# Turning blocks on 128 partitions and placing their squares by a copy through DRAM, in a hybrid decoder layer

## The chip, the cores and the metric

One Trainium2 chip, one core. The metric is the device time of one execution in microseconds. The kernel before was run three times: 1752.36, 1752.54 and 1753.24 us; the median, 1752.54 us, is what the change is measured against.

## The reference

One decoder layer over 256 tokens of width 2048, in float32:

```
h = rmsnorm(x, attn_norm_w)
proj = h @ w_in                      # q,k,v,o and gates of the mLSTM; q,k,v of the attention; two branch gates
hm = sigmoid(mo) * head_rmsnorm(mlstm(silu(conv(q,k)), v, gates))      # 8 heads
hd = head_rmsnorm(diff_attention(dq, dk, dv))                          # 8 heads, causal
y = sigmoid(gm) * (hm @ w_bm) + sigmoid(gd) * (hd @ w_bd)
x = x + y @ w_out
h = rmsnorm(x, ffn_norm_w)
x = x + (silu(h @ w_gate) * (h @ w_up)) @ w_down                       # hidden width 5632
return rmsnorm(x, final_norm_w)
```

## The kernel before

**Products.** All the weights pass through TensorE once, in one stream of products. A product (class `Product`, function `run`) computes 512 columns for all 256 tokens: two PSUM tiles of 128 tokens x 512 columns, over up to 16 row blocks of 128 of the contraction axis. To keep float32 accuracy each operand is split into a high part (rounded to the type fp32r) and a low part, and a row block costs three matmuls per PSUM tile (function `three`): high x high, high x low weights, low x high weights. So a row block is six matmuls of 128 x 128 x 512.

**Weights.** `Feed.load` brings four row blocks (1 MB) by one DMA of SP's queue into one of three raw tiles; `Feed.split` then makes the parts of two row blocks (a unit): a cast on ScalarE (wh, line 254) and a subtraction on VectorE (wl, line 255). Splits are issued four units ahead of the product (`AHEAD = 4`) into five buffers. The next load is issued when a raw tile has been split to its end.

**Steps between the products.** Everything else is cut into generators (class `Side`). After each row block, `run` calls `side.tick()` once: each active generator makes one step, and `yield n` lets n ticks pass before its next step. Every engine's instructions run in the order in which the program stands, so the ticks set the order by hand. Before a row block is multiplied, `side.until` calls further ticks until the left operand's block is marked ready; that settles the program's order, while the engines wait on semaphores in time.

**Blocks across.** A product leaves tokens on partitions; the next product wants the contraction axis there. `across_task` brings a block of 256 tokens x 512 columns across, for each kind either on TensorE (`transpose_task`) or, if its kind is in `TURN`, by `turn_task`. These are in `TURN` and come through `across_task`: hm1 to hm3, dq and dk (four each), hd3, y (the first three), x1 (the first three), x1last, g (the first ones of each of three parts: 3, 3 and 2) and glast4 (the last ones of the parts with four blocks, two of them). That is 29 turns. q0 and k0 use `turn` from `conv_task` and are not touched by the change.

`turn` (line 170 on) transposes on VectorE in squares of 32 x 32. An instruction stays within 32 input and 32 output partitions, so there are 16 of them, `rate` per tick (2, and 4 for x1last and glast4):

```
for n in range(16):
    a, b = n // 4, n % 4
    i = src[32 * a:32 * a + 32].rearrange(...)[:, :, :, b]
    o = t[32 * b:32 * b + 32].rearrange(...)[:, :, :, a]
    nc.vector.transpose(out=o, in_=i)
    if n % rate == rate - 1:
        yield
```

Then `turn_task` splits the turned tile into the high part (ScalarE, line 189, or line 195 where a norm's weight scales it) and the low part (VectorE, line 190 or 196), two row blocks per tick, and marks the block ready.

**Where a block is wanted soonest.** Three places have little room. The last block of x1 (x1last) is made behind the product wo3 and is wanted in row block 12 of the very next product, fg0. The last g of a part (glast4) is made behind fu3 or fu7 and is wanted in row block 12 of the next product, fd00 or fd10. All other turned blocks have at least one whole product in between.

**Queues and buffers.** Weight loads, the loads of x and the output go by SP's queue. POOL only sets constants and copies small columns (lines 694 and 695, at the end of an mv product). The turned tiles, the operands' parts and most other tiles of 128 x 1024 share the 25 buffers of the pool c4p.

Of the kernel before, what the change touches and what calls it, by code (L numbers as in the profile page):

```python
# [15 lines left out]
P = 128  # L16
S = 256
# [19 lines left out]
AHEAD = 4  # L37
ORDER = (
# [8 lines left out]
def hybrid_block(ctx, tc, x, attn_norm_w, w_in, conv_w, conv_b, b_igate, b_fgate, mlstm_norm_w,  # L47
                 lambda_q1, lambda_k1, lambda_q2, lambda_k2, diff_norm_w, w_branch_m, w_branch_d,
                 w_out, ffn_norm_w, w_ffn_gate, w_ffn_up, w_ffn_down, final_norm_w, out):
    """One stream of matrix products on the tensor engine; everything else is cut into steps that are  # L50
    issued between them. Every engine's instructions run in the order in which they stand here."""
# [8 lines left out]
    smp = ctx.enter_context(tc.tile_pool(name="smp", bufs=4))  # L60
    accp = ctx.enter_context(tc.tile_pool(name="accp", bufs=4, space=PS))
# [15 lines left out]
    # ---------------------------------------------------------------- steps between the products  # L77
    class Side:
        """Tasks are generators; each yields the number of further ticks to wait before its next step."""
# [35 lines left out]
    # ---------------------------------------------------------------- operands  # L115
    class Split:
        """An operand with its contraction axis on partitions: [P, 4, S] blocks, high and low parts."""
# [13 lines left out]
    def three(o, a, b, first, last):  # L131
        """o += a.T @ b by the products of their parts."""
        nc.tensor.matmul(o, lhsT=a[0], rhs=b[0], start=first, stop=False)  # L133
        nc.tensor.matmul(o, lhsT=a[0], rhs=b[1], start=False, stop=False)  # L134
        nc.tensor.matmul(o, lhsT=a[1], rhs=b[0], start=False, stop=last)  # L135

    def transpose_half(src, dst, g, pr, scale_col=None):
        """Two [S, 128] column blocks src(tt, j) into dst's row blocks, split."""
# [33 lines left out]
    def turn(src, t, rate=2):  # L172
        """t [P, 4, S] = the transpose of src [P, TT, 512], by blocks of 32 x 32 on the vector engine."""
# [8 lines left out]
    def turn_task(src, dst, g, scale_col=None, rate=2):  # L182
        yield 1
        t = c4([P, 4, S], "turned")
        yield from turn(src, t, rate)
        hi, lo = dst.alloc(g)
        for k in range(0, 4, 2):
            if scale_col is None:
                nc.scalar.copy(out=hi[:, k:k + 2], in_=t[:, k:k + 2])
                nc.vector.tensor_tensor(out=lo[:, k:k + 2], in0=t[:, k:k + 2], in1=hi[:, k:k + 2].bitcast(F32),  # L190
                                        op=ALU.subtract)
            else:
                for j in (k, k + 1):
                    sc = scale_col(4 * g + j)
                    nc.scalar.activation(out=hi[:, j], in_=t[:, j], func=AF.Identity, scale=sc)
                    nc.vector.scalar_tensor_tensor(out=lo[:, j], in0=t[:, j], scalar=sc, in1=hi[:, j].bitcast(F32),
                                                   op0=ALU.mult, op1=ALU.subtract)
            if k == 0:
                yield
        yield  # L200
        dst.ready[g] = True

    # ---------------------------------------------------------------- the products and their weights
    class Product:
        """PSUM tiles [128 tokens, 512] of xt.T @ w[rows of kts, c0:c0+512]; done(acc) takes them."""
# [7 lines left out]
    class Feed:  # L213
        """Loads of four row blocks, then splits of two, in the order of the products."""
# [56 lines left out]
    def run(p):  # L271
# [3 lines left out]
        for tts in ([(0,), (1,)] if p.by_token else [(0, 1)]):  # L275
            for u in p.units:
# [4 lines left out]
                for i, kt in enumerate(kts):  # L281
# [6 lines left out]
                    if p is first and kt == 0:  # L288
                        # in the order in which the parts come
# [12 lines left out]
    # ---------------------------------------------------------------- 1 / sqrt  # L302
    def rsqrt(v, n, name):
        """1 / sqrt(v) on [P, n], by Newton steps from an integer estimate."""
# [32 lines left out]
    # ---------------------------------------------------------------- start: constants, x, first weights  # L337
# [7 lines left out]
    def load_x(c, i, n):  # L345
        """Piece i of n of column chunk c of the tokens."""
# [5 lines left out]
    def x_cols(c, k):  # L352
        """Columns [128 k, 128 k + 128) of chunk c."""
# [15 lines left out]
    mask_st = cp.tile([P, S], F32, name="mask_st")   # keys on partitions, queries along the row  # L369
    mask_ts = cp.tile([P, P], F32, name="mask_ts")   # queries on partitions, keys along the row  # L370
# [18 lines left out]
    def warm_up(n):  # L389
        """Products of zeros: the tensor engine's clock rises only under load."""  # L390
# [57 lines left out]
    # ---------------------------------------------------------------- evictions  # L448
# [6 lines left out]
    def values_of(acc, hi, lo):  # L455
        """The product times the token scale, as high and low parts [P, TT, 2, DV]."""
# [10 lines left out]
    # ---------------------------------------------------------------- gates of the mLSTM  # L467
# [12 lines left out]
    def gates_task():  # L480
# [9 lines left out]
        # columns per row block: [i high | f high | i low | f low], 32 apart  # L490
# [9 lines left out]
        # the token scales along the row  # L500
# [23 lines left out]
        # log sigmoid(z) = min(z, 0) - log(1 + exp(-|z|))  # L524
# [10 lines left out]
        # m_t - b_t = max(0, max over s <= t of (ig_s - b_s))  # L535
# [19 lines left out]
    # ---------------------------------------------------------------- mLSTM  # L555
# [150 lines left out]
    # ---------------------------------------------------------------- branch gates and the first branch  # L706
# [15 lines left out]
    # ---------------------------------------------------------------- lambda  # L722
# [349 lines left out]
```

## Time and profile before

| what | value |
|---|---|
| runs | 1752.36, 1752.54, 1753.24 us |
| profiled execution: span from first to last instruction | 1750.4 us |
| TensorE (PE) busy | 1739.8 us |
| TensorE's weight loads (PEld) busy | 1443.0 us |
| VectorE (DVE) busy | 1217.4 us |
| ScalarE (ACT) busy | 856.6 us |
| GpSimd (POOL) busy | 6.3 us |
| moved by DMA | 332.08 MB |

The page gives the profiled execution by its span alone; the 2.1 us between span and median lie around the first and the last instruction. Busy time counts instructions in execution. Shares are of the span. Matmuls overlap by their pipeline, so the mean of one is longer than the distance between two.

### The profile page before, as it was taken

What the parts mean: (1) busy time and instruction counts of PE and PEld (TensorE: products, weight loads), DVE (VectorE), ACT (ScalarE), POOL (GpSimd) and SP (SyncE); (2) the same over time, 40 slices, a digit from 0 to 9 for tenths busy, and PEclk for the clock granted to TensorE, in tenths of its full rate; (3) what the DMA queues carried; (4) which work ended last, traced back from release to release, by engine and by line L of the source; (5) the groups of instructions that cost most, each with busy time, mean ns of one, the idle gap of its engine ahead of it and who ended that gap; (6) DMA issues with size and microseconds to landing.
All of it is one profiled execution on the core that took longest, in us unless ns stands there. A gap on an engine that the chain in (4) does not pass through costs nothing.

```text
span 1750.4 us, 20353 instructions
## 1 busy us (share of the span) xinstructions
PE 1739.8 (99%) x7873; PEld 1443.0 (82%) x7873; DVE 1217.4 (70%) x1838; ACT 856.6 (49%) x1103; POOL 6.3 (0%) x31
## 2 busy tenths in 40 slices
PE   9999999999999999999999999999999999999998
PEld 7888888888888888888888888888888888888886
DVE  6876877875567978876597886666546666546655
ACT  7555565644345555565444554444344444344443
POOL 1000000000000000000000000000000000000000
PEclk9999999999999999999999999999999999999999
DMA  8656555655666556555666566665566665566553
GB/s 265 215 174 192 163 174 172 180 192 195 193 194 179 175 167 187 169 172 181 212 217 204 192 206 203 193 192 193 193 194 192 194 196 195 194 193 195 196 185 106
DMA packets 169872, 332.08 MB, mean 190 GB/s; under 512 B 7584, under 2 KB 9264, under 8 KB 169776
## 3 DMA queue, kind: packets, MB, share of 16 engines
q1 hardware_dynamic: 169744, 330.78, 59.8%
q8 instruction: 61, 1.00, 0.2%
q14 instruction: 35, 0.29, 0.0%
q10 hardware_dynamic: 32, 0.01, 0.0%
HBM read 328.67 MB, written 2.10 MB: 189 GB/s over the span
## 4 chain that ended last, share of the span: by engine, by line
PE 99%; DMA 0%; DVE 0%; SPq 0%; ACT 0%; issue 0%; DVEq 0%
PE acc_fd L135 5%; PE acc_fg L134 5%; PE acc_fg L133 5%; PE acc_fu L134 5%; PE acc_fu L133 5%; PE acc_fd L133 5%; PE acc_fu L135 5%; PE acc_fg L135 5%; PE acc_fd L134 5%; PE acc_mv L133 2%; PE acc_mo L133 2%; PE acc_dq L133 2%; PE acc_gm L133 2%; PE acc_gd L133 2%; PE acc_dq L135 2%; PE acc_dk L135 2%
## 5 line engine op out<-in xcount | busy, mean ns | idle before, releaser
L255 DVE TENSOR_TENSOR wl_fg<-wr_fg,wh_fg 128x1024 fp32r<-128x1024 f32 x88 | 107.8, 1225 | 85.3 <-ACT wh_fg L254 84.7
L255 DVE TENSOR_TENSOR wl_fu<-wr_fu,wh_fu 128x1024 fp32r<-128x1024 f32 x88 | 107.6, 1225 | 80.8 <-ACT wh_fu L254 80.3
L254 ACT CAST wh_fg<-wr_fg 128x1024 fp32r<-128x1024 f32 x88 | 93.0, 1057 | 142.1 <-PE acc_fu L135 66.5
L255 DVE TENSOR_TENSOR wl_fd<-wr_fd,wh_fd 128x1024 fp32r<-128x1024 f32 x82 | 100.1, 1225 | 89.7 <-ACT wh_fd L254 89.6
L254 ACT CAST wh_fd<-wr_fd 128x1024 fp32r<-128x1024 f32 x82 | 86.2, 1056 | 122.1 <-PE acc_fd L135 96.1
L254 ACT CAST wh_fu<-wr_fu 128x1024 fp32r<-128x1024 f32 x88 | 92.6, 1054 | 96.4 <-PE acc_fg L135 48.5
L133 PE MATMUL acc_fg<-wh_fg,x1Th 128*128 128x512 f32 x352 | 136.9, 389 | 0.0
L134 PE MATMUL acc_fg<-wl_fg,x1Th 128*128 128x512 f32 x352 | 136.9, 389 | 0.0
L135 PE MATMUL acc_fg<-wh_fg,x1Tl 128*128 128x512 f32 x352 | 136.9, 389 | 0.0
L133 PE MATMUL acc_fu<-wh_fu,x1Th 128*128 128x512 f32 x352 | 136.9, 389 | 0.0
L134 PE MATMUL acc_fu<-wl_fu,x1Th 128*128 128x512 f32 x352 | 136.9, 389 | 0.0
L135 PE MATMUL acc_fu<-wh_fu,x1Tl 128*128 128x512 f32 x352 | 136.9, 389 | 0.0
L133 PEld LDWEIGHTS acc_fg<-wh_fg,x1Th 128*128 128x128 f32 x352 | 66.1, 188 | 13.7
L135 PEld LDWEIGHTS acc_fg<-wh_fg,x1Tl 128*128 128x128 f32 x352 | 66.1, 188 | 13.7
L133 PEld LDWEIGHTS acc_fu<-wh_fu,x1Th 128*128 128x128 f32 x352 | 66.1, 188 | 13.7
L135 PEld LDWEIGHTS acc_fu<-wh_fu,x1Tl 128*128 128x128 f32 x352 | 66.1, 188 | 13.7
L134 PEld LDWEIGHTS acc_fu<-wl_fu,x1Th 128*128 128x128 f32 x352 | 66.1, 188 | 13.7
L134 PEld LDWEIGHTS acc_fg<-wl_fg,x1Th 128*128 128x128 f32 x352 | 66.1, 188 | 13.6
L178 DVE STREAM_TRANSPOSE turned<-g 32x256 f32<-32x256 f32 x160 | 69.7, 435 | 2.5
L255 DVE TENSOR_TENSOR wl_bm<-wr_bm,wh_bm 128x1024 fp32r<-128x1024 f32 x32 | 39.2, 1225 | 37.4 <-ACT wh_bm L254 37.3
L178 DVE STREAM_TRANSPOSE turned<-tok_dqk 32x256 f32<-32x256 f32 x128 | 55.7, 435 | 2.1
L254 ACT CAST wh_bm<-wr_bm 128x1024 fp32r<-128x1024 f32 x32 | 33.8, 1056 | 46.6 <-PE acc_bm L135 42.4
(378 smaller groups left out, 4611.4 us busy)
## 6 DMA issues: line engine op xcount, KB each, us to landing
wr_fg<-in_w_ffn_gate_dram SPq DMA_DIRECT2D x44, 1024.0 KB, 5.2
wr_fu<-in_w_ffn_up_dram SPq DMA_DIRECT2D x44, 1024.0 KB, 5.2
wr_fd<-in_w_ffn_down_dram SPq DMA_DIRECT2D x44, 1024.0 KB, 5.1
wr_mo<-in_w_in_dram SPq DMA_DIRECT2D x16, 1024.0 KB, 5.5
wr_mv<-in_w_in_dram SPq DMA_DIRECT2D x16, 1024.0 KB, 5.4
wr_gm<-in_w_in_dram SPq DMA_DIRECT2D x16, 1024.0 KB, 5.4
wr_bm<-in_w_branch_m_dram SPq DMA_DIRECT2D x16, 1024.0 KB, 5.1
wr_dq<-in_w_in_dram SPq DMA_DIRECT2D x16, 1024.0 KB, 5.4
```

The lines of the kernel that those rows point to most:

```text
L133: nc.tensor.matmul(o, lhsT=a[0], rhs=b[0], start=first, stop=False)
L134: nc.tensor.matmul(o, lhsT=a[0], rhs=b[1], start=False, stop=False)
L135: nc.tensor.matmul(o, lhsT=a[1], rhs=b[0], start=False, stop=last)
L178: nc.vector.transpose(out=o, in_=i)
L254: nc.scalar.copy(out=hi[:, i:i + step], in_=r)
L255: nc.vector.tensor_tensor(out=lo[:, i:i + step], in0=r, in1=hi[:, i:i + step].bitcast(F32), op=ALU.subtract)
```

## The change

`turn_task` no longer calls `turn`. It transposes all 128 partitions at once, one instruction per 128 tokens, which turns each 32 x 32 square where it lies: the squares then stand in the wrong groups of 32 partitions. One DMA of POOL's queue writes this tile (4 KB per partition) to a tile in DRAM, and four DMAs of the same queue, one for each group of 32 partitions, read the squares back to their places, in pieces of 1 KB. Seven ticks later (`yield TURN_WAIT`) the parts are made as before; since the squares of one row block now lie 32 elements apart, the cast reads them in that order. Scaled blocks get one more tile: ScalarE scales into it, then casts it, and VectorE subtracts from it. `rate` is no longer used by `turn_task`. The other lines of the change only take out comments.

```
+TURN_WAIT = 6
+    drp = ctx.enter_context(tc.tile_pool(name="drp", bufs=3, space=bass.MemoryType.DRAM))
     def turn_task(src, dst, g, scale_col=None, rate=2):
         yield 1
-        t = c4([P, 4, S], "turned")
-        yield from turn(src, t, rate)
+        y = c4([P, 4, 4, TT, 32], "turned")
+        for tt in range(TT):
+            nc.vector.transpose(out=y[:, :, :, tt].rearrange("p b k s -> p k b s"),
+                                in_=src[:, tt].rearrange("p (k b f) -> p k b f", k=4, f=32))
+            yield
+        d = drp.tile([4, 32, 4, 256], F32, tag="d", name="across")
+        nc.gpsimd.dma_start(out=d.rearrange("a f b n -> (a f) (b n)"), in_=y.rearrange("p b k t s -> p (b k t s)"))
+        t = c4([P, 4, 4 * TT, 32], "across")
+        for b in range(4):
+            nc.gpsimd.dma_start(out=t[32 * b:32 * b + 32].rearrange("p a u s -> p a (u s)"),
+                                in_=d[:, :, b].rearrange("a f n -> f a n"))
+        yield TURN_WAIT
         hi, lo = dst.alloc(g)
+        z = None if scale_col is None else c4([P, 4, S], "scaled")
         for k in range(0, 4, 2):
+            def i(k, n):
+                return t[:, :, TT * k:TT * (k + n)].rearrange("p a u s -> p u a s")
+            def o(x, k, n):
+                return x[:, k:k + n].rearrange("p k (t a s) -> p (k t) a s", t=TT, s=32)
             if scale_col is None:
-                nc.scalar.copy(out=hi[:, k:k + 2], in_=t[:, k:k + 2])
-                nc.vector.tensor_tensor(out=lo[:, k:k + 2], in0=t[:, k:k + 2], in1=hi[:, k:k + 2].bitcast(F32),
-                                        op=ALU.subtract)
+                nc.scalar.copy(out=o(hi, k, 2), in_=i(k, 2))
+                nc.vector.tensor_tensor(out=o(lo, k, 2), in0=i(k, 2), in1=o(hi, k, 2).bitcast(F32), op=ALU.subtract)
             else:
                 for j in (k, k + 1):
-                    sc = scale_col(4 * g + j)
-                    nc.scalar.activation(out=hi[:, j], in_=t[:, j], func=AF.Identity, scale=sc)
-                    nc.vector.scalar_tensor_tensor(out=lo[:, j], in0=t[:, j], scalar=sc, in1=hi[:, j].bitcast(F32),
-                                                   op0=ALU.mult, op1=ALU.subtract)
+                    nc.scalar.activation(out=o(z, j, 1), in_=i(j, 1), func=AF.Identity, scale=scale_col(4 * g + j))
+                nc.scalar.copy(out=hi[:, k:k + 2], in_=z[:, k:k + 2])
+                nc.vector.tensor_tensor(out=lo[:, k:k + 2], in0=z[:, k:k + 2], in1=hi[:, k:k + 2].bitcast(F32),
+                                        op=ALU.subtract)
             if k == 0:
                 yield
         yield
         dst.ready[g] = True
```

## Rows read from the trace of the kernel before

**Rows 1.** The page: busy time, granted clock by slices, chain that ended last

```profile
PE 1739.8 (99%) x7873; PEld 1443.0 (82%) x7873; DVE 1217.4 (70%) x1838; ACT 856.6 (49%) x1103; POOL 6.3 (0%) x31
...
PEclk9999999999999999999999999999999999999999
...
PE 99%; DMA 0%; DVE 0%; SPq 0%; ACT 0%; issue 0%; DVEq 0%
```

**Rows 2.** The waits of TensorE, all: us in total, times, longest

```profile
PE ps_warm L393 <- DVE ssx L387: 1.1, 1, 1.1
PE acc_mq L292 <- ACT wh_mq L254: 0.4, 1, 0.4
PE ps_x L401 <- DMA x<-in_x_dram: 0.2, 1, 0.2
```

**Rows 3.** The turned tile's transposes, of g: duration ns min/median/max, first and last start

```profile
L178 DVE STREAM_TRANSPOSE turned<-g x160: 425/436/442, 1071.1 to 1647.4; 32x256 f32<-32x256 f32 x160
```

**Rows 4.** In time order around the start of fd00 (VectorE, then TensorE): start us, length us

```profile
1200.54 1.23 DVE L255 TENSOR_TENSOR wl_fd<-wr_fd,wh_fd 128x1024 fp32r<-128x1024 f32 x1 [1.50 <-ACT wh_fd L254]
1201.68 3.57 DVE L178 STREAM_TRANSPOSE turned<-g 32x256 f32<-32x256 f32 x8
...
1211.30 1.29 DVE L190 TENSOR_TENSOR gT0l<-turned,gT0h 128x512 fp32r<-128x512 f32 x2
...
1196.53 0.39 PE L133 MATMUL acc_fd<-wh_fd,gT0h 128*128 128x512 f32 x1
...
1212.85 0.39 PE L133 MATMUL acc_fd<-wh_fd,gT0h 128*128 128x512 f32 x1
1213.08 0.39 PE L134 MATMUL acc_fd<-wl_fd,gT0h 128*128 128x512 f32 x1
1213.31 0.39 PE L135 MATMUL acc_fd<-wh_fd,gT0l 128*128 128x512 f32 x1
```

**Rows 5.** Groups by line and shape, ScalarE and VectorE: busy us, mean ns, idle before

```profile
L189 ACT CAST gT0h<-turned 128x512 fp32r<-128x512 f32 x8 | 4.6, 623 | 8.2 <-DVE turned L178 8.2
L195 ACT ACTIVATE x1Th<-turned,nw 128x256 fp32r<-128x256 f32 x16 | 7.0, 501 | 8.3 <-DVE turned L178 8.3
L190 DVE TENSOR_TENSOR gT0l<-turned,gT0h 128x512 fp32r<-128x512 f32 x8 | 5.1, 685 | 0.0
L196 DVE SCALAR_TENSOR_TENSOR x1Tl<-turned,nw,x1Th 128x256 fp32r<-128x256 f32 x16 | 6.7, 480 | 0.0
```

**Rows 6.** In time order around the start of fg0 (VectorE, then TensorE)

```profile
1027.66 3.57 DVE L178 STREAM_TRANSPOSE turned<-x 32x256 f32<-32x256 f32 x8
...
1039.23 0.39 PE L135 MATMUL acc_fg<-wh_fg,x1Tl 128*128 128x512 f32 x1
```

**Rows 7.** DMA: GB/s in 40 slices of 1195 to 1215 us; issues, KB, us to landing

```profile
GB/s 242 0 0 0 20 41 188 418 406 410 406 209 0 0 0 33 20 254 397 401 414 422 156 0 0 0 0 0 0 0 0 0 0 0 16 49 127 397 406 406
...
DMA packets 169872, 332.08 MB, mean 190 GB/s; under 512 B 7584, under 2 KB 9264, under 8 KB 169776
...
x<-in_x_dram SPq DMA_DIRECT2D x6, 512.0 KB, 6.2
...
nwa<-in_attn_norm_w_dram ACTq DMA_DIRECT2D x1, 8.0 KB, 3.0
...
DMA to landing us min/median/max: 2.4/3.1/3.3
```

The last line is that of the eight stores of 256 KB to out_dram, from the view of line 959.

**Rows 8.** What an issue on SP's queue takes (ns), and POOL's instructions, by form

```profile
L237 SPq DMA_DIRECT2D wr_bd<-in_w_branch_d_dram x16: 367/368/368, 827.9 to 908.4; - x16
...
L694 POOL CAST vah<-one 128x4 fp32r<-128x4 f32 x8 | 1.6, 200 | 208.2 <-PE ps_at L135 158.0 <-issue 50.2
...
L484 POOL TENSOR_SCALAR_AFFINE_SELECT sel<-sel 8x1024 f32<-8x1024 f32 x1 | 1.1, 1083 | 0.1
L483 POOL MEMSET sel<- 8x1024 f32 x1 | 0.9, 942 | 0.0
```

**Rows 9.** ScalarE's longest wait in all: us in total, times, longest

```profile
ACT wh_fd L254 <- PE acc_fd L135: 96.1, 59, 1.7
```

## The prediction

> **What bounds the kernel now.** I read the page first, then the waits of the tensor engine, then the turned tile, then the time order at the places where a turned block is needed soonest.
>
> The page's busy line and its chain say one thing: TensorE is busy for 1739.8 of 1750.4 us, and 99% of the chain that ended last is TensorE's own matmuls [rows 1]. VectorE's 70% and ScalarE's 49% lie beside that. TensorE's waits confirm it: three of them in the whole program, 1.7 us together [rows 2]. The clock line grants 9 tenths or more in every slice [rows 1], so there is nothing to win there either. In time order the first matmul of fd00 starts at 1196.53 and the one twelve row blocks later at 1212.85 [rows 4]: 1.36 us for a row block of six matmuls, with no gap. The 10.6 us in which TensorE is idle lie at the start and behind the last matmul, where no block is turned by the code that changes.
>
> So a faster VectorE buys nothing. The change can cost time only by making TensorE wait. The profiled span is 1750.4 us, the median of the runs 1752.54, 2.1 us around it; I add to the median.
>
> **What it removes and adds on the engines.** There are 29 turns in turn_task: 10 of g, 8 of the attention's queries and keys, 4 of x1, 3 of hm, 3 of y, 1 of hd; the ten of g are the 160 transposes of [rows 3]. Each loses 16 transposes of 0.436 us, 6.98 us of VectorE, and gets two of 128 x 512. No row shows such a one. A transpose of 256 columns takes 0.436 us, so 0.87 is the upper bound by doubling; a subtraction of 128 x 512 takes 0.685 [rows 3, 5], the lower. I take 0.7 since the row nearest in shape is the subtraction. That leaves 29 x 5.6 = 161 us less VectorE work, all of it beside TensorE: worth 0. The final casts and subtractions are as many as before, with runs of 32 elements; I cost them as now. For the 8 scaled turns (hm, hd, x1) ScalarE writes a scaled tile first (0.50 us per row block, [rows 5]) and then copies it, two more casts of 0.62 us per turn, while VectorE has two subtractions of 0.69 in place of four of 0.48. Covered by the idle ScalarE, except at x1last, below.
>
> **What it adds on the path of the data.** Between the transposes and the cast there is now a store of 512 KB to DRAM and four loads of 128 KB, all five on POOL's queue; the loads wait there for the store. POOL's queue holds little else: the small copies of vah and val at the end of an mv product, which come 12 row blocks or more ahead of the next turn's transfers. SP's queue issues nothing for it, but the weight loads share the 16 DMA engines with it: 30 MB more on 332 MB [rows 7].
>
> How long may this trip, R, take? A block of the last product before a new stage is needed soonest: glast4 (twice) and x1last. The tick order is exact in the code. The task yields once, transposes at the ticks of row blocks 2 and 3, issues the transfers at 4, waits TURN_WAIT = 6 and casts from row block 11; TensorE needs the result at row block 12, and a deadline of 12 holds in time as well.
> - glast4: VectorE reaches the transposes at 1201.68 [rows 4]; two of 0.7 end at 1203.1. Row block 12 starts at 1212.85 and its third matmul, the first that reads the low part, at 1213.31. After the landing come a cast of 0.62 and a subtraction of 0.69 [rows 5]. R is free up to 1213.31 - 1.31 - 1203.1 = 8.9 us. Before, the low parts came at 1211.30 to 1212.59 [rows 4], already only 0.7 us ahead.
> - x1last: transposes from 1027.66, so ended at 1029.06; the third matmul of row block 12 at 1039.23 [rows 6]. Behind the landing lie two scalings (0.50 each), a cast of 0.62, a subtraction of 0.69 [rows 5]: 2.3 us. R is free up to 1039.23 - 2.3 - 1029.06 = 7.9 us.
>
> Each us beyond is a us of TensorE, since nothing else can fill it: cost = 2(R - 8.9) + (R - 7.9) = 3R - 25.7.
>
> **R from both sides.** POOL has not issued a transfer in this trace. Store: 256 KB took 3.1 us from issue to landing (2.4 at least), alone [rows 7]; 256 KB more at the 400 GB/s that the DMA engines reach [rows 7] is 0.65, so 3.75. A weight load of 1 MB runs in bursts of 2.6 us; in the window of glast4 one runs from 1203.5 to 1206.3 [rows 7], over the store, and sharing with it adds up to 1.3 us. At x1last the final norm's weights and a weight load do the same. So 5.05. Loads: 8 KB landed after 3.0 us [rows 7], 128 KB adds 0.3; the four are issued in line, so three issues come ahead of the last. SP takes 0.37 us for an issue [rows 8]; POOL writes its own descriptors, and its costliest instructions here take 0.94 and 1.08 us [rows 8]. I take 0.7, between the two, as POOL is neither. Store 5.05 + 0.35 (the dearer issue) = 5.4; three issues 2.1; last load 3.3 + 0.35 + 0.65 (half a collision with the next weight load, which VectorE now releases sooner, at about 1207) = 4.3. R = 11.8. Lowest: 3.75 + 3 x 0.37 + 3.3 = 8.2, no collision and SP's issue. Highest: two transfers behind a weight load as the 512 KB load of x (6.2, [rows 7]), POOL's 1.08 for each of five issues: 6.2 + 6.2 + 5 x 1.08 = 17.8.
>
> The Trainium skill, "DMA: Bandwidth & Descriptors", section "Anatomy of one DMA — SWDGE (gpsimd) path", fits such a transfer by 2.0 us plus bytes at 436 GB/s. By it the store is 3.2, a last load 2.3, and with three issues R would be near 7 and the sum 0. The trace's 3.1 for 256 KB, where the fit gives 2.6, speaks against the fit as a whole.
>
> The sum: 3 x 11.8 - 25.7 = 9.7 us. 1752.5 + 9.7 = **1762.2 us**.
>
> **Why the other 26 turns cost nothing.** ScalarE and VectorE work in program order, so a cast that waits for its landing holds the weight splits behind it. These run four units ahead: ScalarE waits for TensorE to release the buffer 59 times, 96.1 us, in fd alone [rows 9]. Four units are 8 row blocks, 10.9 us, less the 2.3 of a split itself: a stall of some 8 us passes, and ScalarE at half load catches up. At R = 11.8 the cast of a turn waits about 3 us. The blocks themselves are needed a whole product (16 row blocks, 21.8 us) or more after the product that made them: dk's before the scores behind dv (R up to about 16), y[0..2], x1[0..2] and the other g's later still. If R passed 17 these covers go too.
>
> **Rivals.**
> 1. *Hidden.* R is at most 9.7, so the three waits sum to no more than 3.5 us: 1752.5 to 1756. For it: the lowest bound of 8.2, and the burst that ends at 1206.3 need not meet the store. Against: three issues and two receipts in sequence. It decides at fd00 and fd10 (R = 8.9). 0.25. The Trainium skill's fit, above, lies here.
> 2. *POOL starved.* VectorE's instructions hold up the writing of descriptors: each of five issues waits for a 1.23 us subtraction of wl (1.50 us idle ahead of one, [rows 4], so not always). Full price 6.1 us on R: 3 x 17.9 - 25.7 = 28 us, 1780; half of it 1771. For it: VectorE runs one every 2.7 us at these places. Against: POOL's small copies in this trace take 0.2 us each [rows 8], no stretch. 0.13. The Trainium skill, "SBUF — State Buffer", section "Who interferes with whom", has the shared port between the two; it holds that two-input subtractions block only POOL's reads, which would make this cheap. No run so far shows which.
> 3. *Buffers.* y, the returned tile and, where scaled, one more tile come from the 25 c4 buffers. By count 23 are live at glast4, up to 24 in the attention stage: a load might wait for a buffer. Some us at most; 0.03, within the range.
> 4. *Faster.* Only TensorE's 1.7 us of waits could go, and none lies on this code: 0.02.
>
> **Numbers.** A measurement of this kernel can tell about 0.2%, 3.5 us. Forecast 0.57, hidden 0.25, starved 0.13, buffers 0.03, faster 0.02: faster 0.02, same 0.25, slower 0.73. The range goes from the hidden case's floor, 1752.2, to R = 15.5 (half of rival 2, or the upper bound cut by a third of its way), 3 x 15.5 - 25.7 = 20.8, 1773.5. The likeliest case alone: R from 9.7 to 13.5, 1756 to 1767.5.
>
> **What would show it.** In the profile after: two transposes of 128 x 512 near 0.7 us per turn, VectorE's busy time down by about 160 us; POOL's queue with 145 issues; in TensorE's waits three entries for x1Tl, gT0l and gT1l of 2 to 5 us each, and next to none elsewhere; ScalarE's casts waiting for a DMA named across. Wrong, if TensorE still shows 1.7 us of waits (then R is under 9), if its waits lie in the weights wh or wl (then the covers are gone), or if the transfers land late because POOL's issues spread by more than 1 us each.

## The result and the profile after

After: 1802.88 us, the median of three runs (1797.91 to 1806.84); before 1752.54. The ratio is 1.0284 with an interval of 1.0256 to 1.0311. The forecast was 1762.2 with a range up to 1773.5: the sign is right, and the loss is 50 us where 9.7 were forecast.

The page of after, whose profiled span is 1801.1 us: busy time, granted clock by slices, chain that ended last.

```profile
PE 1754.3 (97%) x7873; PEld 1451.1 (81%) x7873; DVE 1048.9 (58%) x1416; ACT 856.5 (48%) x1119; POOL 85.9 (5%) x176
...
PEclk9999999999999999999999999999999999999999
...
PE 77%; issue 11%; DMA 7%; ACT 2%; DVE 1%; POOL 1%; SPq 0%; ACTq 0%; DVEq 0%; POOLq 0%
```

VectorE lost 168.5 us of work [rows 1], about the 161 forecast, and the kernel gained nothing from it. DMA and "issue" have come into the chain, where TensorE alone stood before. TensorE itself is busy 14.5 us longer with the same 7873 matmuls. Its waits, all of 2 us and more and one of the small ones (us in all, times, longest), for the three entries of [rows 2]:

```profile
PE acc_fg L135 <- ACT x1Th L216: 11.6, 1, 11.6
PE acc_fd L135 <- ACT gT0h L211: 7.6, 1, 7.6
PE ps_tr L145 <- DVE sgd L873: 4.0, 2, 3.0
PE acc_fd L135 <- ACT gT1h L211: 2.8, 1, 2.8
PE acc_fg L135 <- ACT wh_fg L275: 2.6, 1, 2.6
PE ps_at L624 <- DVE nm L628: 2.3, 1, 2.3
PE ps_at L135 <- ACT dkh L211: 2.0, 1, 2.0
...
PE acc_fg L136 <- DVE wl_fg L276: 0.8, 1, 0.8
```

With the other small entries they make 37.9 us, 36.2 more than before. 36.2 of waits and 14.5 of longer matmuls are the 50.7 us between the spans, 1801.1 - 1750.4; nothing is left over. The three urgent blocks (x1Th, gT0h, gT1h) are the first, second and fourth line, 22.0 us. The other 14.2 us lie, but for 0.8 at the start, where the prediction had cost nothing: at weights (wh_fg, wl_fg, wl_gd), at the y transposes (sgd), in the mLSTM (nm) and the attention (dkh).

The 14.5 us are TensorE's clock: its mean over the execution is 0.999 before and 0.989 after, and 0.010 of 1801 us would be some 18 us (an estimate; part of that lies in the waits themselves). Stretches of after behind the waits at fg0 and fd00; the columns are PE, PEld, DVE, ACT and POOL busy (instructions), granted clock, DMA share, GB/s:

```profile
1072.00:1076.00 4.00, 2.99 (x7) 2.37 (x8) 2.52 (x3) 3.30 (x6) 0.00 (x0) 0.50 0.00 0
1076.00:1080.00 4.00, 4.00 (x18) 3.25 (x18) 1.31 (x2) 2.43 (x3) 0.00 (x0) 0.98 0.02 4
1256.00:1260.00 4.00, 3.53 (x8) 2.78 (x9) 2.52 (x3) 1.89 (x3) 0.00 (x0) 0.50 0.00 0
```

When TensorE came back from 11.6 and from 7.6 us of idleness, the granted clock was 0.50, 1.2 GHz of 2.4: seven matmuls in 3.0 busy us and eight in 3.5, where the row after fg0's holds eighteen in 4.0. The 40 slices of the page, 45 us each, don't show it; only narrow windows do.

The turned tile and its trip, from the views of the transposes' line and of the two issue lines: duration in ns min/median/max, first and last start; under the loads, us from issue to landing. They answer to [rows 3, 8].

```profile
L190 DVE STREAM_TRANSPOSE turned<-g x20: 669/686/705, 1107.0 to 1688.1; 128x512 f32<-128x512 f32 x20
...
L195 POOL DMA_DIRECT2D across<-turned x29: 558/558/740, 258.0 to 1689.1; - x29
...
DMA to landing us min/median/max: 4.9/6.0/7.2
...
L198 POOL DMA_DIRECT2D across<-across x116: 550/550/562, 265.4 to 1696.5; - x116
...
DMA to landing us min/median/max: 2.8/4.5/8.3
```

At fd00 and fg0, in time order (start, length), for [rows 4, 6]; POOL, then ScalarE, then TensorE:

```profile
1239.12 0.56 POOL L195 DMA_DIRECT2D across<-turned  x1 [34.19 <-DVE turned L190]
1244.73 1.10 POOL L198 DMA_DIRECT2D across<-across  x2 [5.05 <-ACT wh_fd L275]
1248.19 1.10 POOL L198 DMA_DIRECT2D across<-across  x2 [2.37 <-issue]
...
1255.80 0.62 ACT L211 CAST gT0h<-across 128x512 fp32r<-128x512 f32 x1 [8.57 <-DMA across<-across]
...
1256.47 0.80 PE L135 MATMUL acc_fd<-wh_fd,gT0h 128*128 128x512 f32 x1 [7.61 <-ACT gT0h L211]
...
1029.79 0.56 POOL L195 DMA_DIRECT2D across<-turned  x1 [17.51 <-DVE turned L190]
...
1045.16 0.91 ACT L215 ACTIVATE scaled<-across,nw 128x256 f32<-128x256 f32 x2 [12.57 <-DMA across<-across]
...
1056.31 0.56 POOL L195 DMA_DIRECT2D across<-turned  x1 [18.98 <-DVE turned L190]
...
1071.40 0.91 ACT L215 ACTIVATE scaled<-across,nw 128x256 f32<-128x256 f32 x2 [11.57 <-DMA across<-across]
```

From the store's issue to the first cast or scaling: 16.7 us at fd00, 15.1 at fg0. The lines at 1029.79 and 1045.16 are one of the 26 other turns, x1[2]: ScalarE stood 12.6 us waiting for its landing, then did four weight casts in one run (3.9 us from 1049.0), SP's loads followed in a bunch, and the DMA engines ran at about 400 GB/s nearly throughout 1055 to 1067 us, just when x1last's trip had to pass. Here one trip delays the next by way of the splits.

The same lines show a second effect. At fd00 ScalarE was at its cast 8.1 us behind the store's issue (1255.80 - 8.57 - 1239.12). At x1[2] it was catching up after the hold of the turn before (7.8 us, until 1018.6), ran through the splits in between faster than TensorE uses them, and was at its scaling only 2.8 us behind the issue: of a trip of 15.4 us it waited 12.6. A tick is a place in the order and not a time.

ScalarE's waits for landings (us in all, times, longest) show that this was no single case. Rows 5's casts had waited for transposes; these wait for the DMA:

```profile
ACT scaled L215 <- DMA across<-across: 60.4, 8, 12.6
ACT dkh L211 <- DMA across<-across: 25.7, 4, 11.1
ACT gT0h L211 <- DMA across<-across: 20.4, 4, 8.6
ACT dqh L211 <- DMA across<-across: 18.6, 4, 7.7
ACT yTh L211 <- DMA across<-across: 17.8, 3, 9.5
ACT gT1h L211 <- DMA across<-across: 15.7, 4, 4.9
ACT gT2h L211 <- DMA across<-across: 6.7, 2, 3.4
```

29 waits, one for every turn, 165.3 us: the six ticks of `TURN_WAIT` (the cast comes on the seventh) were too few for each of them. Of the 26 turns that are not urgent, 17 held ScalarE for 3.2 to 4.9 us, and no wait of TensorE follows these. The small waits of TensorE follow five of the nine holds of 6.2 us and more (hm 6.4, dk 11.1, hd 7.4, y 9.5, x1[2] 12.6).

### The profile page after: what moved, and what is told of

Read it like the earlier page. It is cut to its first block, busy times and chain, and to the rows that moved or that the text cites. A ratio compares the mean times of both kernels' runs of the same rounds, so it can differ in the third digit from the quotient of the medians.

```text
span 1801.1 us, 20295 instructions
## 1 busy us (share of the span) xinstructions
PE 1754.3 (97%) x7873; PEld 1451.1 (81%) x7873; DVE 1048.9 (58%) x1416; ACT 856.5 (48%) x1119; POOL 85.9 (5%) x176
## 4 chain that ended last, share of the span: by engine, by line
PE 77%; issue 11%; DMA 7%; ACT 2%; DVE 1%; POOL 1%; SPq 0%; ACTq 0%; DVEq 0%; POOLq 0%
PE acc_fu L136 4%; PE acc_fu L137 4%; PE acc_fu L135 4%; PE acc_fd L135 4%; PE acc_fd L137 4%; PE acc_fd L136 4%; PE acc_fg L135 4%; PE acc_fg L136 4%; PE acc_fg L137 4%; DMA across<-across 3%; DMA across<-turned 3%; PE acc_mo L135 2%; PE acc_mo L137 2%; PE acc_mo L136 2%; PE acc_bd L135 1%
## 5 line engine op out<-in xcount | busy, mean ns | idle before, releaser
L135 PE MATMUL acc_fg<-wh_fg,x1Th 128*128 128x512 f32 x352 | 138.6, 394 | 14.2 <-ACT x1Th L216 11.6
L195 POOL DMA_DIRECT2D across<-turned x29 | 16.4, 565 | 1416.6 <-DVE turned L190 1416.6
L135 PEld LDWEIGHTS acc_fu<-wh_fu,x1Th 128*128 128x128 f32 x352 | 66.1, 188 | 13.7
L137 PEld LDWEIGHTS acc_fu<-wh_fu,x1Tl 128*128 128x128 f32 x352 | 66.1, 188 | 13.7
L198 POOL DMA_DIRECT2D across<-across x116 | 63.2, 552 | 175.5 <-DMA across<-turned 97.5
L135 PE MATMUL acc_fd<-wh_fd,gT0h 128*128 128x512 f32 x128 | 50.8, 397 | 7.6 <-ACT gT0h L211 7.6
```

The costliest lines, as they stand in the source:

```text
L195: nc.gpsimd.dma_start(out=d.rearrange("a f b n -> (a f) (b n)"), in_=y.rearrange("p b k t s -> p (b k t s)"))
L198: nc.gpsimd.dma_start(out=t[32 * b:32 * b + 32].rearrange("p a u s -> p a (u s)"), in_=d[:, :, b].rearrange("a f n -> f a n"))
```

## The experiments

The theories on record before the first four runs: A, a trip of some 15 us is paid where its block is wanted in the next product, by casts held behind a landing, and by half the clock behind each wait; B, the extra traffic or POOL's queue slows the weight loads everywhere; C, the strided casts and the scaled tile cost. The table holds what before, after and the thirteen kernels of the experiments gave: the median, the ratio to before with its interval, TensorE's busy time and waits in the profiled run, and ScalarE's waits for landings of "across". The profiled run of e5 is one of its longest (1758.0 us), that of e11 took 1759.8.

| kernel | us | ratio [interval] | TensorE busy, us | its waits, us | ScalarE's waits for landings, us (times) |
|---|---|---|---|---|---|
| before | 1752.5 | | 1739.8 | 1.7 | |
| after | 1802.9 | 1.0284 [1.0256, 1.0311] | 1754.3 | 37.9 | 165.3 (29) |
| e1 three old | 1782.6 | 1.0169 [1.0147, 1.0192] | 1748.7 | 21.0 | 148.0 (26) |
| e2 eleven ticks | 1774.6 | 1.0128 [1.0113, 1.0143] | 1746.1 | 18.3 | 19.4 (5) |
| e3 both | 1752.6 | 1.0003 [0.9993, 1.0012] | 1740.3 | 2.1 | 2.5 (2) |
| e4 no trip | 1753.5 | 1.0008 [0.9999, 1.0018] | 1741.2 | 1.7 | none |
| e5 direct copies | 1754.0 | 1.0018 [1.0008, 1.0027] | 1742.3 | 5.1 | 5.3 (2) |
| e6 SP's queue | 1762.6 | 1.0061 [1.0046, 1.0076] | 1743.1 | 10.7 | 14.7 (6) |
| e7 filled waits | 1774.0 | 1.0123 [1.0106, 1.0140] | 1758.3 | 7.4 | 24.4 (4) |
| e8 quiet trips | 1752.3 | one run | 1739.8 | 1.9 | 0.6 (1) |
| e9 four more | 1758.0 | 1.0035 [1.0022, 1.0047] | 1739.2 | 7.7 | 19.8 (4) |
| e10 q1, k1 too | 1768.0 | 1.0088 [1.0074, 1.0101] | 1741.7 | 15.7 | 34.7 (7) |
| e11 eight ticks | 1760.8 | 1.0059 [1.0035, 1.0083] | 1742.5 | 6.6 | 64.4 (25) |
| e12 direct, POOL | 1764.0 | 1.0066 [1.0052, 1.0080] | 1745.4 | 7.7 | 11.5 (6) |
| e13 twenty ticks | 1748.8 | 0.9980 [0.9971, 0.9989] | 1736.5 | 1.6 | 2.1 (1) |

**Which turns cost (e1 to e4).** e1 turns the three urgent blocks by the old sixteen transposes; e2 lengthens the wait of the 26 others; e3 does both; e4 leaves the five transfers out.

```diff
-        if kind in TURN:
+        if kind in LAST:                      # e1: x1last, glast4
+            yield from old_turn_task(tile, dst, g, scale_col, rate)
+        elif kind in TURN:
             yield from turn_task(tile, dst, g, scale_col, rate)
```

> The three last turns (x1last, glast4 twice) use the old sixteen transposes again, the other 26 keep the trip through DRAM. Theory A (the trip is some 15 us long; it is paid where a block is wanted in the next product, by ScalarE's casts held behind a landing, and by the half clock after each wait): the waits of 25 us at fg0, fd00 and fd10 and their half clock go; left are the waits elsewhere (mlstm, ylast, dk, about 10 us) and two short stretches at half clock, about 5 us: 1764 to 1770 us. Theory B (the extra traffic and POOL's queue slow the weight loads everywhere): nearly all of the loss stays, 1790 us or more.

Measured: 1782.6, above what A had for it and below B's. A's mechanism stands, its size does not: the 26 turns held to be covered cost 28.2 us of span by themselves (1778.6 - 1750.4), 19.3 of waits and 8.9 of longer matmuls.

```diff
-            yield from turn_task(tile, dst, g, scale_col, rate)
+            yield from turn_task(tile, dst, g, scale_col, rate, TURN_WAIT if kind in LAST else 11)
...
-        yield TURN_WAIT
+        yield wait
...
-            side.push("tr", across_task("x1" if c < 3 else "x1last", t, x1T, c, ffn_col, 2 if c < 3 else 4))
+            side.push(f"tr{c}", across_task("x1" if c < 3 else "x1last", t, x1T, c, ffn_col, 2 if c < 3 else 4))
```

(y and the attention's queries and keys get a lane per task in the same way.)

> The trip for all 29 turns, but the 26 that are not last ones wait 11 ticks more instead of 6 before their casts, and turns that would overlap in a lane get lanes of their own. Theory A: the waits outside fg0, fd00 and fd10 go, and at fg0 the wait is shorter since x1's third turn no longer pushes the last one back: three waits of 3 to 8 us with the half clock after each, 1772 to 1784 us. Theory B: no change, 1795 us or more.

Measured: 1774.6. Of TensorE's waits only the three urgent ones are left besides those at the start, with 9.9 (x1Th), 4.6 (gT0h) and 2.3 us (gT1h). So the urgent turns alone cost 22 us (against e3, below): 16.8 of waits, some 6 of half clock. With e1's 28.2 that is nearly the whole of the 50.7.

> Both: the old transposes for the three last turns, the trip with 11 ticks for the other 26. Theory A: no wait of TensorE is left but the 1.7 us of before, 1751 to 1755 us, with VectorE some 145 us less busy than before: the relief is worth nothing. Theory B: 1775 us or more, since the traffic is as in the change but for a tenth.

Measured: 1752.6, the time of before, with 26 trips and 27 MB of extra traffic in it. B falls.

```diff
-        d = drp.tile([4, 32, 4, 256], F32, tag="d", name="across")
...
-        yield TURN_WAIT
+        t = y.rearrange("p b k t s -> p b (k t) s")
+        yield TURN_WAIT
```

> The change without its five transfers: the casts read the tile that the two transposes wrote, so the squares are not placed (that part of the computation is left out). Everything else as in the change, with the strided casts and the extra scaled tile. Theory A: 1751 to 1755 us, as the kernel before. A theory C, that the strided casts or the extra scaled tile cost: 1760 us or more.

Measured: 1753.5. C falls, and with it any worth of the relief: VectorE at 1053.6 us and not 1217.4 [rows 1] leaves the time where it was.

**How long must the wait be (e11).** e3 with 8 in place of 11.

> As the run with the old form of the three urgent turns and eleven ticks of wait for the others, with eight ticks in place of eleven. A trip takes 11.4 to 16.3 us in the traces, eight ticks are 10.9 us behind the store's issue, eleven are 15.0. Theory A (what the 26 covered turns cost at six ticks, 8.2 us, is ScalarE and VectorE held behind landings that come after the tick, and the splits queued behind them): at eight ticks most holds are a few us and inside the splits' lead, 1752 to 1760 us. Rival H (not the length of the wait but the separate lanes took the cost of six ticks away): 1752 to 1753.5 us, as at eleven.

Measured: a median of 1760.8, in runs from 1752.9 to 1776.7; A's range ended at 1760. Rival H falls, since the lanes are e3's: the ticks count. ScalarE's waits for landings are 148.0, 64.4 and 2.5 us at 6 (e1), 8 and 11 ticks. Six ticks with the lanes were not run, so what the lanes gave of the step from e1 to e11 is not shown. At eight, whether a landing comes in time differs from run to run, and the time with it.

**Why the trip is long (e5, e6, e8, e12).** e5 takes e2 and moves the squares of the three urgent turns in one hop; e6 takes e2 and issues the three urgent trips on SP's queue; e8 puts two trips that nothing reads into e3, behind the last weight loads; e12 is e5 with another share of the queues.

```diff
+        if direct:
+            for a in range(4):
+                for b in range(4):
+                    queue = nc.gpsimd if b < 2 else nc.sync
+                    queue.dma_start(out=t[32 * b:32 * b + 32, a].rearrange("p u s -> p (u s)"),
+                                    in_=y[32 * a:32 * a + 32, b].rearrange("p k t s -> p (k t s)"))
```

> As the run with eleven ticks of wait, but in the three turns that the next product wants (the last x1 and the two last g) the squares go straight from the turned tile to their places in on-chip memory, by sixteen copies of 32 KB (eight on POOL's queue, eight on SP's) and not by a store to DRAM and four loads behind its landing: one landing in place of two. In the run with eleven ticks these three trips took 16.3, 13.7 and 11.4 us from the store's issue to the first cast that reads the squares, and TensorE waited 9.9, 4.6 and 2.3 us for them. Theory A (the length of the trip, two landings one behind the other, is what the three products wait for): one landing of 4 to 6 us behind issues of 3 to 4.4 us makes 8 to 10 us, which the 7.9 to 8.9 us of free room nearly hold; waits of 0 to 2 us each, 1752 to 1762 us. Rival B (the two queues' many small copies land as late as the trip, since the weight loads hold the DMA engines): 1770 us or more.

Measured: 1754.0, in A's range (runs from 1753.9 to 1758.1). In the profiled one, of 1758.0, fd00 and fd10 no longer wait; 3.3 us are left at fg0, more than A's 0 to 2, where the first scaling starts 10.6 us behind the first copy's issue.

> As the run with eleven ticks of wait, but the three turns that the next product wants have their store and loads issued on SP's queue, not on POOL's. Rival D (the trip is long because POOL prepares its descriptors itself: in the traces POOL stands 2.4 us between two loads of one trip, and waits about 5 us for the store): the trip falls to 10 us or less and the time to 1762 us or less. Theory A (the trip is two landings beside weight loads that fill the DMA engines, whichever queue issues it): 12 us or more each, 1770 to 1780 us; SP's weight loads behind the waiting loads then come up to 5 us later, which the splits' lead of four units (10.9 us) holds.

Measured: 1762.6, between the two, at D's edge. The trips fell from 16.3, 13.7 and 11.4 us to 12.7, 10.3 and 10.4; this is fg0's (SP, then ScalarE), with the loads' KB and median us to landing at fg0, first e6's, then e2's:

```profile
1031.90 0.33 SPq L197 DMA_DIRECT2D across<-turned  x1
1040.33 1.76 SPq L200 DMA_DIRECT2D across<-across  x4
...
1044.56 0.91 ACT L217 ACTIVATE scaled<-across,nw 128x256 f32<-128x256 f32 x2 [6.95 <-DMA across<-across]
...
across<-across SPq DMA_DIRECT2D x4, 128.0 KB, 2.8
...
across<-across POOLq DMA_DIRECT2D x4, 128.0 KB, 5.4
```

A trip is 2.7 us shorter on the mean of the three, but that is not the price of POOL's queue. The stores landed no sooner on SP: after 8.4, 5.9 and 6.0 us (fg0, fd00, fd10), where e2's took 8.7, 4.9 and 4.9. The loads did, after 2.8 to 2.9 us and not 5.4, 4.4 and 4.3. SP's next weight loads stood in the queue behind these loads (at fg0 they were issued at 1042.19), so the loads hardly shared the DMA engines. This rival to D was not tested by a run of its own. Even here fg0's store takes 8.4 us before its loads can be issued.

> The run with the old form of the three turns and eleven ticks of wait for the others, and two more trips of a 512 KB tile that nothing reads, after the last weight load has landed (in the trace of before the DMA engines move nothing from about 1719 to 1737 us): one issued on POOL at about 1720 us, one on SP at about 1736 us. It measures a trip by itself. Theory A (a good part of the 11.4 to 16.3 us is shared DMA engines): 8 to 10 us from the store's issue to the last landing on either queue, stores of 3 to 4.5 us. Rival D (POOL's own preparation is what is long): 11 us or more on POOL, and 3 us or more shorter on SP. The time stays at 1751 to 1758 us.

Measured: the two issue lines of the loads ("still" is the tile they fill), first POOL's, then SP's.

```profile
L962 POOL DMA_DIRECT2D still<-across x4: 552/553/557, 1721.5 to 1723.1; - x4
L972 SPq DMA_DIRECT2D still<-across x4: 346/425/432, 1731.8 to 1733.1; - x4
...
DMA to landing us min/median/max: 2.8/2.9/2.9
```

POOL's store was issued at 1715.1 and landed after 6.1 us; its last load landed at 1723.1 + 2.9 = 1726.0: 10.9 us. SP's store was issued at 1729.0, so 2.8 us passed until its loads: 1733.1 + 2.9 - 1729.0 = 7.0 us. So a bare trip is 7 us on SP, and some 4 us more come with the weight loads beside it (e6's mean of 11.1), as A says in kind; its 8 to 10 us on either queue met neither trip. The 10.9 us look like rival D, but POOL's trip was not a bare one: its store shared the DMA engines with the last weight load, of 1 MB, for most of its 6.1 us, and 3.6 of the 3.9 us between the two trips lie ahead of the loads. The loads, on quiet engines, landed after 2.8 to 2.9 us on both queues, and the shortest of POOL's stores in e2 took 3.1 us. What these runs show of POOL's queue by itself is an issue every 0.55 us where SP's come every 0.43.

```diff
-                    queue = nc.gpsimd if b < 2 else nc.sync
+                    queue = nc.gpsimd if b < 3 else nc.sync
```

> As the run with direct copies for the three urgent turns (1754.0 us, where TensorE waits 3.3 us at fg0 and nothing at fd00 and fd10), with twelve of the sixteen copies on POOL's queue and four on SP's, not eight and eight: at fg0 SP took 8.1 us to issue its eight beside the weight loads, POOL 3.9 us for its eight. Theory A (the trip ends where the slower queue's last copy lands): POOL needs 5.9 us and SP about 4, the trip falls from 10.5 us to 8 to 9, the wait at fg0 to 0 to 1.5 us and the time to 1751.5 to 1753 us. Rival I (the landing of the copies beside the weight loads sets it, whoever issues): 1754 us as before it.

Measured: 1764.0, 10 us worse than e5 and outside what either had. At all three places POOL issued eight of its copies and then waited for a landing (1.2, 0.7 and 0.6 us); here at fd00:

```profile
1208.93 3.95 POOL L200 DMA_DIRECT2D across<-turned  x8 [34.55 <-DVE turned L191]
1213.61 1.47 POOL L200 DMA_DIRECT2D across<-turned  x3 [0.74 <-DMA across<-turned]
1217.87 0.50 POOL L200 DMA_DIRECT2D across<-turned  x1 [2.80 <-issue]
```

The last copy goes out at 1217.9, 8.9 us behind the first, 2.8 of them in a gap with no releaser in the profile. The waits that e5 had removed at fd00 and fd10 are back (1.7 and 1.6 us). But at fg0 and fd10 the last copy went out 6.6 and 6.0 us behind the first, about A's 5.9, and TensorE still waited 3.3 and 1.6 us. So the hold explains a part of the cost at fd00 at most; the rest stays open.

**Is the longer busy time the clock (e7).**

```diff
+                    if kt - p.k0 == 12 and p.name in FILL:
+                        ps = trp.tile([P, 512], F32, tag="tr", name="ps_fill")
+                        for _ in range(FILL[p.name]):
+                            nc.tensor.matmul(ps, lhsT=p.xt.get(0, 0)[0], rhs=hi[:, i], start=True, stop=True)
```

> As the run with eleven ticks of wait, but TensorE is given products of no use (the first x block by the waiting row block's weights, into a PSUM tile that nobody reads) just before the three row blocks that wait: 42 before fg0's, 18 before fd00's and 8 before fd10's, some 0.227 us each by the rate of the rows, so 9.5, 4.1 and 1.8 us in place of waits of 9.9, 4.6 and 2.3 us. Theory A's third part (of the 22 us by which that run is above the run with the old form of the three turns, 16.8 are waits and some 5 to 6 are row blocks at 1.2 GHz behind the waits): the stretches at half clock go, and the time falls by 3 to 6 us, to 1768 to 1772 us. Rival E (the half clock does not come from the idle stretch, or the filling makes the casts later): no gain, 1774 us or more.

Measured: 1774.0, no gain, as rival E had it; yet the clock did what A said. Windows of e7 behind the waits that were left at fg0, fd00 and fd10, 3.7, 1.6 and 0.6 us (columns as above); in e2 the granted clock in such windows was 0.83, 0.76 and 0.66:

```profile
1052.00:1065.00 13.00, 13.00 (x50) 10.37 (x51) 6.25 (x6) 8.06 (x11) 0.00 (x0) 0.87 0.26 81
1234.00:1241.00 7.00, 7.00 (x31) 5.49 (x30) 4.79 (x7) 3.19 (x4) 0.00 (x0) 1.00 0.09 6
1498.00:1503.00 5.00, 5.00 (x22) 3.80 (x22) 3.09 (x4) 2.25 (x3) 0.00 (x0) 1.00 0.28 110
```

Without its 68 useless matmuls (9.68, 4.24 and 1.97 us in the three places) TensorE is busy 1758.3 - 15.9 = 1742.4 us, 3.7 less than e2. But the trip at fg0 took 20.2 us and not 16.3, and the one at fd00 14.7 and not 13.7: waits of 3.7 and 1.6 us came on top of the filling. This is the second half of rival E, casts made later; its first half, a half clock that does not come from the idle stretch, falls at fd00 and fd10. Why the landings came later was not tried.

**Do covered turns cost anything by themselves (e9, e10, e13).** Four tiles that before turns on TensorE go to the new form.

```diff
-TURN = {"q0", "k0", ...}
+TURN = {"hm0", "hd0", "hd1", "hd2", "q0", "k0", ...}     # e10: and "q1", "k1", by the old sixteen
```

> The run with the old form of the three urgent turns and eleven ticks of wait for the others (1752.6 us), and four tiles more turned by the new form with eleven ticks: hm0, hd0, hd1 and hd2, which before turns by eight TensorE transposes each and whose readers come long after. In before's trace four such transposes push the matmuls behind them back by 0.44 us (0.36 and 0.08), so 32 of them hold TensorE for 8 x 0.44 = 3.5 us. Theory A (a trip costs nothing where its reader comes later than it lands, and TensorE is the bound): 1748 to 1750 us, faster than before. Rival F (four more trips make the weight loads or the casts late in the attention stages): 1752 us or more.

Measured: 1758.0, slower than e3 and than before, and in F's range. The trace names why. POOL, then ScalarE, around hd's turn:

```profile
594.62 0.56 POOL L219 DMA_DIRECT2D across<-turned  x1 [18.14 <-DVE turned L214]
601.24 2.19 POOL L222 DMA_DIRECT2D across<-across  x4 [6.06 <-DMA across<-turned]
603.41 0.56 POOL L219 DMA_DIRECT2D across<-turned  x1
612.13 2.19 POOL L222 DMA_DIRECT2D across<-across  x4 [8.15 <-PE acc_dq L138]
...
620.10 0.91 ACT L239 ACTIVATE scaled<-across,nw 128x256 f32<-128x256 f32 x2 [5.15 <-DMA across<-across]
```

hd's transposes were done at 600.5, but its store stood on POOL behind dk's four loads, which waited for dk's store (2.9 us), and then took 8.7 us itself: 19.6 us to the scaling, more than eleven ticks hold.

> As the run with four tiles more, and the two tiles q1 and k1 of the convolution turned by the old sixteen vector transposes and not by eight TensorE transposes each: by the same 0.44 us per four, 4 x 0.44 = 1.8 us less of TensorE, for 2 x 16 x 0.436 = 14 us more of VectorE, which stands idle for more than half of the time. Theory A: 1746 to 1748 us. Rival G (VectorE's work between 170 and 230 us makes its subtractions late and TensorE waits): no gain over the run with four more, or 1750 us and more.

Measured: 1768.0, the time that rival G had, but mostly by another way. TensorE's waits doubled to 15.7 us, 5.9 of them for VectorE's pt in the mLSTM, where q1 and k1 are used. ScalarE, VectorE and TensorE there:

```profile
281.05 0.91 ACT L239 ACTIVATE scaled<-across,nw 128x256 f32<-128x256 f32 x2 [9.65 <-DMA across<-across]
282.64 0.69 DVE L241 TENSOR_TENSOR hmTl<-scaled,hmTh 128x512 fp32r<-128x512 f32 x1 [9.27 <-ACT hmTh L240]
288.37 0.58 PE L136 MATMUL ps_at<-q1h,k1h 128*128 128x256 f32 x1 [5.85 <-DVE pt L661]
```

VectorE itself stood idle for 9.3 us ahead of pt, behind a trip of hm. What its added work did was to make hm's transposes late: the store went out 7.7 us ahead of ScalarE's arrival at the scaling, where e9 has 14.1 us for the same turn. Subtractions of weights that came late, G's own way, cost 1.4 us (wl_mv). VectorE's average idleness was no room there.

```diff
-            yield from turn_task(tile, dst, g, scale_col, rate, TURN_WAIT if kind in LAST else 11)
+            yield from turn_task(tile, dst, g, scale_col, rate, 20 if kind in LONG else 11)
```

> As the run with four tiles more (1758.0 us), with twenty ticks and not eleven between the copies' issue and the casts for hm0, hd0, hd1 and hd2 (their readers come 100 us later and more). In that run the four copies of dk, waiting on POOL for their store, held hd's store back by some 3 us, and hd's own copies landed 20 us and more behind its transposes, so that ScalarE stood 18 us in three waits for them and TensorE 6.4 us for probabilities that come out of the same engines. Theory A (a covered trip costs only what ScalarE and VectorE are held behind its landing; twenty ticks are 27 us): the waits go, and what is left is TensorE's 3.5 us less of transposes: 1748 to 1750.5 us, faster than before. Rival F (the trips' traffic or the two more tiles that each holds cost in the attention stages by themselves): 1754 us or more.

Measured: 1748.8, ratio 0.9980 [0.9971, 0.9989], in A's range and 0.2% faster than before; the interval lies below 1. TensorE's waits and busy time:

```profile
PE ps_warm L439 <- DVE ssx L433: 1.1, 1, 1.1
PE ps_x L447 <- DMA x<-in_x_dram: 0.5, 1, 0.5
```

```profile
PE 1736.5 (99%) x7841; PEld 1440.4 (82%) x7841; DVE 1070.0 (61%) x1460; ACT 867.5 (50%) x1125; POOL 88.7 (5%) x181
```

With 30 trips in it TensorE waits no more than before, and its busy time is 3.3 us less than before's [rows 1], for 32 transposes that left it (3.5 expected). Here a trip whose landing comes ahead of its cast costs nothing.

## Why the prediction was wrong, step by step

- *TensorE is the bound, a faster VectorE is worth 0*: right. e4 has the relief without the trip, and the time of before.
- *Two transposes at 0.7 us*: right, 0.686.
- *Three urgent places and their free room (8.9, 8.9, 7.9 us)*: right to about 1 us where nothing was held before. In e2 the trips, counted from the transposes' ends as the formula does, were 14.0 (fd00), 11.7 (fd10) and 16.6 us (fg0): 42.3 - 25.7 = 16.6, and the three waits measured 16.8. That this is so close is partly luck: less their waits, the trips had 9.4, 9.4 and 6.7 us of room. In after the room at fg0 was only 3.8 us (15.4 - 11.6), since x1[2]'s hold had made x1last's transposes late.
- *R = 11.8*: the first term mis-sized. It is 14.1 on the mean of e2's three, up to 16.6, and in after 15.4 at fg0 and 17.0 at fd00 (the range closed at 15.5). At e2's fd10 it was 11.7, with a store of 4.9 us (5.4 forecast) and loads of 4.3 (4.3 forecast). At e2's fg0 the store took 8.7 and the loads 5.4 us beside the weight loads: there the prices for sharing, 1.3 us on the store and 0.65 on a load, were too low. At fd00 2.4 us are a gap between POOL's loads that no term had. The bare trip, 7.0 us on SP (e8), lies below the forecast's lowest, 8.2. In after the stores took 4.9 to 7.2 us and loads up to 8.3. The Trainium skill, "DMA: Bandwidth & Descriptors", section "Anatomy of one DMA — SWDGE (gpsimd) path", whose fit gives 3.2 us for the store, is further off for stores beside weight loads: POOL's 29 have a median of 6.0. The shortest of e2's, 3.1, comes near it. The prediction's row against the fit, 3.1 us for 256 KB, was one of SP's queue.
- *"There is nothing to win there either"*, of the clock: true of before, but the price of a wait was then taken as its length. Each long wait also sent TensorE back at 1.2 GHz: 14.5 us in after, 8.9 in e1, some 6 in e2. This term was missing; e7 shows that it goes where the idle stretch is filled.
- *"Why the other 26 turns cost nothing"*: the step that failed most, 28 us (e1). The lead of some 8 us was about right: holds of up to 4.9 us cost TensorE nothing in after. What failed is the hold itself, 3 us in the forecast: the casts stood 5.7 us on the mean (165.3 / 29) and up to 12.6. The trips were longer than 11.8, and behind one hold ScalarE came to the next cast sooner (2.8 us behind the issue at x1[2]); there the hold also sent the weight loads in a bunch against the next trip. The sentence "If R passed 17 these covers go too" put the bound at the reader's need; it lies at the place of the cast, 8.1 us behind the issue at fd00, and some 8 us of lead further, since ScalarE and VectorE hold the weights' splits behind it: by an estimate from these rows a trip of some 15 us where nothing was held before, and less behind a hold. e3 shows it the other way round: three more ticks than e11, and the cost is gone.
- *Rivals*: hidden falls with R. POOL starved falls for the issues: one took 0.550 us at the median and 0.562 at most in 116, beside a VectorE that was busy for 58% of the span; the Trainium skill, "SBUF — State Buffer", section "Who interferes with whom", by which two-input subtractions leave POOL's writes alone, agrees with that row. The one gap of 2.4 us between two loads (fd00) is unexplained. What POOL's queue was seen to cost is order (e9) and the hold behind eight copies (e12). Buffers: nothing shows. Faster: not this change, though e13 gets there with its parts.
- The forecast's own test, "if its waits lie in the weights wh or wl (then the covers are gone)", came true: 2.6 and 0.8 us at wh_fg and wl_fg.

## What to carry to other kernels

Where engines run in program order, a transfer is surely free only if it has landed when its consumer's turn comes in that order. That its reader is far off does not help, since what stands behind the consumer waits too; a late landing passes only as far as the lead of that work reaches (here 17 holds of up to 4.9 us did, the longest did not). Price a trip through DRAM from transfers that run beside the real traffic, by the longest and not the median, and give the consumer that many ticks and some more, since an engine that catches up passes its ticks faster. And to the length of each long TensorE wait add the row blocks that follow at half clock.

## What the runs showed of the hardware that was not expected

- The granted clock stood at 0.50 behind waits of 11.6 and 7.6 us, and averaged 0.66 over the 5 us behind e2's wait of only 2.3 us; with matmuls of no use in two of the waits it stayed at 1.00 (e7).
- POOL issued eight copies in a row and held the ninth until one had landed (e12); the eight copies that SP issued beside the weight loads at fg0 took 8.1 us of its queue, where eight at fd00 and fd10 took 5.0 (e5) and four took 2.4 to 2.5 (e12).
- POOL's issue of a 512 KB store, 0.56 us, and its four loads, 0.55 us each, didn't vary with size or, but for a single 0.74, from one to the next; but a gap of 2.4 us with no releaser in the profile stands between two loads of one trip at fd00 in after, e2 and e7 alike, and at one turn of g in e3. What it is stays open.
- Four loads of 128 KB landed after 2.8 to 2.9 us where the DMA engines were quiet or the weight loads stood behind them (e8, e6), and after 4.3 to 5.4 us beside weight loads (e2).
